# Feed-forward parts with quarter products: the weight steps are handed out more densely, up to four at a time

## The chip, the cores and the metric

The kernel runs as one program on 1 core of a Trainium2 chip. The metric is the device time of one execution in microseconds; the time shown of a kernel is the median of three executions. All numbers are float32; the matrix products are made of three matmuls each (high parts by high parts, low by high, high by low).

## The reference

512 tokens of width 1024 (16 more meta tokens stand ahead of them in the first block) go through two blocks: one with two layers, each with a feed-forward part, a mixer of attention and a gated recurrence, and a second feed-forward part; then one with a state space branch, an attention with a top-k choice, and a feed-forward part. What the change touches are four of the five feed-forward parts:

```python
D_MODEL = 1024; SEQ = 512; DEPTH = 2; N_META = 16; D_FF = 2816

def swiglu(x, w_gu, w_down):
    gate, up = jnp.split(x @ w_gu, 2, axis=-1)
    return (jax.nn.silu(gate) * up) @ w_down

for l in range(DEPTH):
    h = h + 0.5 * swiglu(rms_norm(h, ffn1_norm[l]), ffn1_w_gu[l], ffn1_w_down[l])   # a0, a1
    ...                                                                             # the mixer
    h = h + 0.5 * swiglu(rms_norm(h, ffn2_norm[l]), ffn2_w_gu[l], ffn2_w_down[l])   # b0, b1
...                                                                                 # the second block
x = x + (jax.nn.silu(h2 @ w_ffn_gate[l]) * (h2 @ w_ffn_up[l])) @ w_ffn_down[l]      # c
```

## The kernel before

Activations lie transposed: eight tiles `h` of 128 features by 528 tokens (512 in b1 and c). The hidden width of a feed-forward part is 22 slices of 128, called j = 0 to 21. For one slice the gate weights (1024 by 128) and the up weights are a chunk of 512 KB each; the down weights of a third of the slices (8, 7 and 7) and 128 outputs are a chunk of 512 or 448 KB. Chunks land in `raw` tiles, of which there are four (`RAW`, L285); a chunk is asked for when the fourth before it has been used up (`drop`).

Part a0 and the slices 0 to 5 of the others use plain products. In b0, a1, b1 and c the slices 6 to 21 are done by seven products of quarter size (`product`, L608): the two weight blocks are cut in halves over their inputs, and gate and up of one slice come out of seven products of four 128 by 128 weight tiles each, 12 matmuls of 264 (or 256) columns. The seven use three PSUM banks: b1 takes the products 0, 2, 4 and 6, b2 the product 1, b3 the products 3 and 5, each adding onto what stands there. Between two of them the bank is read out ("evacuated"): after product 0 and 2 ScalarE copies b1 to `tu`, after 3 it copies b3 to `zu`, after 1 and 5 VectorE adds into `c1`, after 4 and 6 into `c2`. So the bank of product i must have been read when product i+2 begins. After product 5 a Silu of `c1` follows, after product 6 two multiplications by it and a split of the result into `gh` (ScalarE) and `gl` (VectorE).

The products need sums and differences of weight halves, and all weights need a split into a high part `whi` (ScalarE) and a low part `wlo = w - whi` (VectorE here). This work is cut in steps (`steps_of`, L374): eleven for one slice, in this order: hi0a+s1, hi0b+s3, lo0, a2, hi1a+s4 (drops the gate chunk), hi1b+lo1a, hi2a+lo1b, hi2b+lo2a, lo2b, hi3, lo3 (drops the up chunk); and two, hi and lo, for a down chunk. The names: s1, s3, s4 and a2 are sums of 512 columns on VectorE, hi and lo are the splits of the weight sums 0 to 3 in halves a and b of 512 columns (lo0 takes 1024 at once). The split weights stand in a ring of five pairs of tiles (`H`, L284): the steps of the entry i may begin when the entry i-5 has been used by its last matmul (`allowed`, L425).

In the four parts the order on each engine is pinned: what is written first runs first. The list of the work is fixed: slices 6 and 7, then the slices 8 to 14 woven with the eight down parts of the first third, then 15 to 21 woven with those of the second third; the first four and the last four products of each such run stand alone. A down part is taken apart into items of one 128 by 128 weight tile, three matmuls of 512 columns or six of 264. After the matmuls of each product or item, and ahead of its evacuation, `between` is called (L436): the item's cost (1.46 or 0.73) is added to a credit, and as long as the credit is at least 1 and the ring allows it, the next step is written and takes 1 from the credit. Silu and the split of the slice before are written behind the first of these steps. Outside the four parts no credit is added, and steps run as far ahead as the ring allows.

Of the kernel before, what the change touches and what calls it, by code (L numbers as in the profile page):

```python
# [281 lines left out]
class Kernel:  # L282
# [46 lines left out]
    def run(self):  # L329
# [10 lines left out]
        credit = 0.0  # L340
# [84 lines left out]
        def allowed():  # L425
            if n_step == len(queue):
                return False
            i = queue[n_step][0]
            return i < self.H or done[i - self.H]

        def step():
            nonlocal n_step
            queue[n_step][1]()
            n_step += 1

        def between(cost):  # L436
            nonlocal credit
            credit = min(credit + cost / 0.9, 3.0)
            late, self.late = self.late, []
            while credit >= 1.0 and allowed():  # L440
                step()
                credit -= 1.0
                while late:
                    late.pop(0)()
            for fn in late:
                fn()
# [8 lines left out]
        for it in self.prog:  # L455
            if not (it.seven and self.pin):
                for i in range(used):
                    done[i] = True
            self.pin = it.seven
            if not it.seven:  # L460
                between(0.0)
                if it.chunks:
                    while allowed():
                        step()
            used += len(it.chunks)
            while n_step < len(queue) and queue[n_step][0] < used:
                assert allowed()
                step()
            it.fn()
# [1612 lines left out]
```

## Time and profile before

| | |
|---|---|
| median of three executions | 3180.65 us (3179.32 to 3181.38) |
| the profiled execution's own time | 3182.89 us |
| its span, first to last instruction | 3181.1 us |
| mean granted TensorE clock | 0.992 |
| TensorE busy | 3117.0 us (98%) |
| VectorE busy | 2074.8 us (65%) |
| ScalarE busy | 1378.3 us (43%) |
| GpSimd busy | 853.5 us (27%) |
| moved by DMA | 289.61 MB |

The profile is of one execution. PE is the matmul stream of TensorE, DVE is VectorE, ACT is ScalarE. Nearly all instructions carry the line of one helper (L249), so groups are told apart by the names of their tiles: `bank<-T2h,whi` is a matmul into PSUM. In the products T2h stands for the products 2 and 6, T1h for 3 and 4, B21h for 1 and 5, b11h for 0; `bank<-gh,...` are the down parts. Idle time behind an arrow is what the instruction waited for, and whose end it was. The duration of a matmul covers its way through the array; matmuls follow one another at a closer distance than that.

### The profile page before, as it was taken

How to read it: one execution, taken by the hardware profiler on the slowest of the kernel's cores; microseconds unless marked ns; L12 is line 12 of the kernel's file. 1: busy time of each engine (PE TensorE's matmuls, PEld its weight loads, DVE VectorE, ACT ScalarE, POOL GpSimd, SP SyncE). 2: the span in 40 equal slices, each digit the busy share in tenths (PEclk: the TensorE clock that was granted, in tenths of full speed). 3: DMA queues.
4: the chain of work that ended last, by engine and by line, in shares of the span. 5: the costliest groups of instructions: out<-in, count | busy, mean ns of one | idle time of the engine just before them, and what ended most of it. 6: DMA issues, size and time to landing. Idle time of an engine off the chain costs nothing. (4 is left out here: it accounts for less than half of the span.)

```text
span 3181.1 us, 52632 instructions
## 1 busy us (share of the span) xinstructions
PE 3117.0 (98%) x21530; PEld 2870.7 (90%) x21530; DVE 2074.8 (65%) x3552; ACT 1378.3 (43%) x2355; POOL 853.5 (27%) x493
## 2 busy tenths in 40 slices
PE   9999999999999999999999999999999989999999
PEld 9999999899999999999998888888998767888888
DVE  8664466763676667766666674577667795577674
ACT  5322345544344444444444553444446425444442
POOL 3453235543220002100034453330003543230001
PEclk9999999999999999999999999999999989999999
DMA  6333321111222233223332112222235332222332
GB/s 203 120 99 108 94 94 57 45 58 61 93 80 89 91 101 111 69 94 97 94 109 74 41 51 69 86 93 86 94 106 164 115 96 67 73 93 73 99 103 91
DMA packets 106530, 289.61 MB, mean 91 GB/s; under 512 B 23088, under 2 KB 32304, under 8 KB 106288
## 3 DMA queue, kind: packets, MB, share of 16 engines
q1 hardware_dynamic: 106288, 286.24, 28.5%
q8 instruction: 169, 2.77, 0.4%
q14 instruction: 73, 0.60, 0.1%
HBM read 272.96 MB, written 13.24 MB: 90 GB/s over the span
## 5 line engine op out<-in xcount | busy, mean ns | idle before, releaser
L249 POOL TENSOR_TENSOR wlo<-raw,whi 128x1024 fp32r<-128x1024 f32 (+1 forms) x217 | 542.7, 2503 | 1962.5 <-ACT whi L249 1665.4
L249 ACT ACTIVATE whi<-raw 128x1024 fp32r<-128x1024 f32 (+2 forms) x632 | 537.9, 866 | 813.5 <-PE bank L249 421.5
L249 PE MATMUL bank<-xh,whi 128*128 128x264 f32 (+1 forms) x2504 | 812.7, 325 | 5.3 <-DVE t L249 5.3
L249 PE MATMUL bank<-xl,whi 128*128 128x264 f32 (+1 forms) x2504 | 811.1, 324 | 4.7 <-DVE xl L249 4.4
L249 PE MATMUL bank<-xh,wlo 128*128 128x264 f32 (+1 forms) x2504 | 804.8, 322 | 1.3 <-POOL wlo L249 1.3
L249 PEld LDWEIGHTS bank<-xh,whi 128*128 128x128 f32 x2504 | 475.0, 190 | 35.6 <-DVE t L249 5.7
L249 PEld LDWEIGHTS bank<-xl,whi 128*128 128x128 f32 x2504 | 475.4, 190 | 34.8 <-DVE xl L249 6.6
L249 PEld LDWEIGHTS bank<-xh,wlo 128*128 128x128 f32 x2504 | 474.9, 190 | 26.9 <-issue 1.7
L249 PE MATMUL bank<-gh,wlo 128*128 128x264 f32 (+1 forms) x1408 | 440.6, 313 | 12.1 <-DVE wlo L249 12.1
L249 DVE TENSOR_TENSOR wlo<-raw,whi 128x1024 fp32r<-128x1024 f32 (+2 forms) x351 | 367.8, 1050 | 123.7 <-ACT whi L249 121.3
L249 PE MATMUL bank<-gh,whi 128*128 128x264 f32 (+1 forms) x1408 | 439.8, 312 | 0.0
L249 PE MATMUL bank<-gl,whi 128*128 128x264 f32 (+1 forms) x1408 | 439.7, 312 | 0.0
L249 PEld LDWEIGHTS bank<-gh,wlo 128*128 128x128 f32 x1408 | 265.3, 188 | 30.2 <-DVE wlo L249 14.6
L249 PEld LDWEIGHTS bank<-gl,whi 128*128 128x128 f32 x1408 | 265.3, 188 | 8.3
L249 PEld LDWEIGHTS bank<-gh,whi 128*128 128x128 f32 x1408 | 265.2, 188 | 8.4 <-issue 0.4
L249 ACT ACTIVATE p<-p,nm 128x144 f32<-128x144 f32 (+8 forms) x104 | 57.0, 548 | 227.3 <-DVE nm L249 222.4
L249 PE MATMUL bank<-T2h,whi 128*128 128x264 f32 (+1 forms) x512 | 146.5, 286 | 3.8 <-DVE c L249 3.5
L249 DVE SCALAR_TENSOR_TENSOR h<-bank,h 128x264 f32<-128x264 f32 (+1 forms) x192 | 88.7, 492 | 92.6 <-PE bank L249 91.6
L249 PE MATMUL bank<-T2h,wlo 128*128 128x264 f32 (+1 forms) x512 | 145.8, 285 | 1.8 <-DVE wlo L249 1.8
L249 PE MATMUL bank<-B21h,whi 128*128 128x264 f32 (+1 forms) x512 | 145.5, 284 | 0.9 <-ACT zu L249 0.9
L249 PE MATMUL bank<-B21h,wlo 128*128 128x264 f32 (+1 forms) x512 | 145.1, 283 | 0.0
L249 PE MATMUL bank<-T1h,wlo 128*128 128x264 f32 (+1 forms) x512 | 144.9, 283 | 0.0
(373 smaller groups left out, 6637.9 us busy)
## 6 DMA issues: line engine op xcount, KB each, us to landing
raw<-in_w_dram SPq DMA_DIRECT2D x423, 512.0 KB, 3.5
raw<-in_w_dram SPq DMA_DIRECT2D x80, 448.0 KB, 3.3
h<-in_x_dram SPq DMA_DIRECT2D x8, 264.0 KB, 6.0
s_t<-zero SPq DMA_DIRECT2D x8, 256.0 KB, 3.6
s_wo<-cm SPq DMA_DIRECT2D x16, 128.0 KB, 3.2
s_win<-cm SPq DMA_DIRECT2D x8, 256.0 KB, 2.0
s<-s_win SPq DMA_DIRECT2D x8, 256.0 KB, 4.4
s<-s_wo SPq DMA_DIRECT2D x8, 256.0 KB, 2.9
```

Of the source, the lines that this page charges most:

```text
L249: i = f(*args, **kw)
```

## The change

The divisor of the cost goes from 0.9 to 0.65, and the ceiling of the credit from 3 to 4. A product earns 1.46/0.65 = 2.25 steps and not 1.62, an item of a down part 1.12 and not 0.81, and after a time in which the ring allowed nothing up to four steps are written in one place and not three. The instructions are the same ones; what changes is where the steps stand among the evacuations.

```diff
         def between(cost):
             nonlocal credit
-            credit = min(credit + cost / 0.9, 3.0)
+            credit = min(credit + cost / 0.65, 4.0)
             late, self.late = self.late, []
             while credit >= 1.0 and allowed():
                 step()
```

## Rows read from the trace of the kernel before

**Rows 1.** The page's first part: busy us, share of the span, instructions by engine.
```profile
PE 3117.0 (98%) x21530; PEld 2870.7 (90%) x21530; DVE 2074.8 (65%) x3552; ACT 1378.3 (43%) x2355; POOL 853.5 (27%) x493
```
**Rows 2.** Waits of TensorE over the whole span: total us, times, longest.
```profile
PE bank L249 <- DVE wlo L249: 13.8, 16, 1.8
...
PE bank L249 <- DVE c L249: 3.5, 4, 0.9
```
**Rows 3.** Windows over b0 and c: busy PE, PEld, DVE, ACT, POOL; clock; DMA; GB/s.
```profile
960.00:1235.00 275.00, 270.33 (x2187) 268.51 (x2187) 180.34 (x305) 117.40 (x211) 7.00 (x3) 0.99 0.31 96
...
2880.00:3145.00 265.00, 260.45 (x1769) 239.07 (x1768) 179.75 (x290) 115.57 (x210) 7.13 (x3) 1.00 0.32 100
```
**Rows 4.** Waits of TensorE in c, 2880 to 3145 us.
```profile
PE bank L249 <- DVE wlo L249: 3.1, 4, 1.4
...
PE bank L249 <- DVE c L249: 0.8, 1, 0.8
...
PE bank L249 <- ACT zu L249: 0.4, 1, 0.4
...
PE bank L249 <- ACT tu L249: 0.2, 1, 0.2
```
**Rows 5.** Timeline of TensorE in c: start, us, instruction, idle before and releaser.
```profile
2944.33 0.50 PE L249 MATMUL bank<-gh,wlo 128*128 128x512 f32 x1 [1.45 <-DVE wlo L249]
...
3024.43 0.28 PE L249 MATMUL bank<-B21h,wlo 128*128 128x256 f32 x1
3025.53 0.38 PE L249 MATMUL bank<-T2h,whi 128*128 128x256 f32 x1 [0.82 <-DVE c L249]
3025.75 0.28 PE L249 MATMUL bank<-T2l,whi 128*128 128x256 f32 x1
```
**Rows 6.** Groups of VectorE in c by form: busy us, mean ns.
```profile
L249 DVE TENSOR_TENSOR wlo<-s,whi 128x512 fp32r<-128x512 f32 x45 | 29.3, 683 | 5.8 <-ACT whi L249 5.8
L249 DVE TENSOR_TENSOR wlo<-raw,whi 128x1024 fp32r<-128x1024 f32 x23 | 28.1, 1220 | 7.7 <-ACT whi L249 7.7
...
L249 DVE TENSOR_TENSOR wlo<-raw,whi 128x896 fp32r<-128x896 f32 x10 | 10.8, 1084 | 1.5 <-ACT whi L249 1.4
```
**Rows 7.** Groups of ScalarE in c by form.
```profile
L249 ACT ACTIVATE whi<-raw 128x512 fp32r<-128x512 f32 x61 | 36.2, 624 | 33.5 <-PE bank L249 18.1 <-issue 10.2 <-DVE raw L249 4.8
...
L249 ACT ACTIVATE whi<-raw 128x896 fp32r<-128x896 f32 x13 | 12.2, 945 | 6.9 <-DMA raw<-in_w_dram 5.4 <-PE bank L249 1.5
```
**Rows 8.** Timeline of VectorE in c, ahead of product 6 of slice 14.
```profile
3020.91 0.69 DVE L249 TENSOR_TENSOR wlo<-raw,whi 128x512 fp32r<-128x512 f32 x1 [2.76 <-ACT whi L249]
3021.52 0.68 DVE L249 TENSOR_TENSOR s<-raw 128x512 f32<-128x512 f32 x1
...
3023.32 1.22 DVE L249 TENSOR_TENSOR wlo<-raw,whi 128x1024 fp32r<-128x1024 f32 x1
3024.46 0.68 DVE L249 TENSOR_TENSOR raw<-s,raw 128x512 f32<-128x512 f32 x1
3025.06 0.42 DVE L249 TENSOR_TENSOR c<-bank,zu 128x256 f32<-128x256 f32 x1
```
**Rows 9.** Timeline of ScalarE and VectorE at the first product of c.
```profile
2889.66 0.63 ACT L249 ACTIVATE gh<-t 128x512 fp32r<-128x512 f32 x1 [5.35 <-DVE t L249]
2890.20 0.61 ACT L249 ACTIVATE whi<-raw 128x512 fp32r<-128x512 f32 x1
2890.33 0.69 DVE L249 TENSOR_TENSOR gl<-t,gh 128x512 fp32r<-128x512 f32 x1 [0.70 <-ACT gh L249]
2890.72 0.36 ACT L249 ACTIVATE tu<-bank 128x256 f32<-128x256 f32 x1
```
**Rows 10.** Windows around the longest stall of b0; columns as in the windows above.
```profile
1021.00:1024.00 3.00, 1.21 (x10) 0.99 (x9) 2.21 (x3) 2.59 (x6) 0.00 (x0) 1.00 0.01 3
1024.00:1028.00 4.00, 4.00 (x23) 4.00 (x22) 3.32 (x7) 1.58 (x2) 0.00 (x0) 0.57 0.74 262
1028.00:1032.00 4.00, 4.00 (x35) 4.00 (x34) 2.17 (x3) 1.02 (x2) 0.00 (x0) 1.00 0.29 69
```

## The prediction

> **What bounds the kernel now.** I read the page's busy shares first. TensorE is busy 3117.0 of 3181.1 us [rows 1], so what is left to win is its idle time, and of that only what lies where the credit is used. The waits of TensorE come next: 13.8 us for `wlo` and 3.5 us for `c` are the groups that belong to the quarter products [rows 2]. In part c alone they are 3.1 + 0.8 + 0.4 + 0.2 = 4.5 us in seven stalls [rows 4]; four such parts make 18, so the two groups lie wholly in them. The windows say the same: 270.3 of 275 us busy in b0, 260.5 of 265 in c, with VectorE at 66 to 68% and ScalarE at 43 to 44% [rows 3]. So neither helper engine lacks throughput; what counts is how long an evacuation stands in a queue.
>
> A stall costs more than its idle time. Before product 6 of slice 14 the idle time is 0.82, while the starts lie 1.10 and then 0.22 apart, where 0.12 is the usual distance (3025.75 less one) [rows 5]: 1.10 + 0.22 - 0.24 = 1.08, that is 0.27 more than the idle. For c that makes 4.5 + 7 x 0.27 = 6.4 us, for the four parts about 25. That is the most that any order of the steps could give back.
>
> **The change: what it can't touch.** The number of steps is the same, and steps were not short before. In a run of woven work 49 products and 64 items earn 49 x 1.62 + 64 x 0.81 = 131 steps, and 7 x 11 + 8 x 2 = 93 are there. So most of the time the ring holds the next step back, and the credit sits at its ceiling. Counting both kernels through item by item, no step is ever written at the last moment, and a step that waits for the ring is written behind the same matmul in both. The two long `wlo` stalls of each part (1.45 us at 2944.33 [rows 5], and 1.79 in b0 [rows 10]) are of this kind: the third down part of a third takes the ring place of the second, its hi and lo begin only after the last matmul of the second, and one product lies between. They stay.
>
> **What it moves.** A step that is written earlier stands ahead of an evacuation that it stood behind. On ScalarE a hi of 512 columns takes 0.62 us [rows 7] and the next begins 0.54 after its start (2889.66 to 2890.20 [rows 9]); on VectorE a split or sum takes 0.68 [rows 6] and the next begins 0.60 to 0.61 later (3020.91 to 3021.52), a lo of 1024 columns holds the queue for 1.14 (3023.32 to 3024.46 [rows 8]). An evacuation has the time of one product when products stand alone: 12 x 0.12 = 1.43 us. With down items between there is twice that, so the woven stretch has cover (0.1 to 0.3 in a few places). The places without it are the 18 products of slices 6, 7 and the first of 8, and slice 14's end with slice 15's beginning.
>
> Product 6 of slice 14, all four parts. VectorE's queue ahead of `c2` is now lo3, s1, the update of h, s3, lo0, a2 [rows 8], and TensorE waits 0.82. With up to four steps behind the last item, s3 goes ahead of h, and the next products take lo0 with a2, then s4 with lo1a: two more ahead of `c2`, 2 x 0.60 and some 0.1 of waiting for the hi. The stall grows by 1.3 to 1.4.
>
> Product 2 of slice 15, all four. The same slide puts d1.0's lo (1.08 [rows 6]) behind its hi (0.95 [rows 7]) ahead of product 5's `c1`; Silu, the two multiplications, `gh`, and then a hi3 follow before product 0's `tu`. From the end of `c2` that is about 5.2 us, the products take 4.3: 0.9 to 1.0 new.
>
> The beginning. From a1 on a credit of nearly 1 is left from the part before (0.98; in the kernel before 0.49), so product 0 writes three steps: hi0a comes between the hi at 2890.20 and `tu` [rows 9], 0.54 later. Then product 2's `tu` falls behind hi1a, which needs a2. VectorE comes to that from 2890.33 by gl, lo3, s1, s3, lo0, c1, a2: 4 x 0.60 + 1.14 + 0.34 + 0.68 = 4.6, to 2894.9; hi1a and `tu` end at 2895.9. Product 4 could start at 2891.14 + 0.54 + 0.11 + 2 x 1.43 = 2894.65: 1.25 lost, where nothing was. Product 2 of slice 7 loses 2.0: the pair of multiplications of slice 6 stands behind lo3, c1, s1, s3 and lo0 (3.3 us and about 1.3 of waits for their hi), and `tu` behind the `gh` that follows. In b0, which begins with credit 0, it is 0.9 and 0.75 before products 5 and 6 of slice 6 and 0.3 there. Product 2 of slice 8 loses 0.4 more in c, 0.7 in b0 (its `tu` behind a `gh` that comes late).
>
> The sum. I laid out the three queues of each part in issue order with these durations, both ways. New less old, in us: b0 0.9 + 0.75 + 0.3 + 0.1 + 0.7 + 1.4 + 0.9 - 0.1 = 4.9; a1 0.5 + 1.3 + 0.1 + 2.0 - 0.1 + 0.45 + 1.4 + 0.9 - 0.15 = 6.4; b1 and c each 0.5 + 1.4 + 0.1 + 2.1 - 0.5 (a wait for `zu` that goes) + 0.4 + 1.4 + 1.0 + 0.6 in the woven stretch = 7.0. Together 25.3. Laid out so, the kernel before loses 31 us, where the rows give some 25, so the sum may be a fifth too large: 20 to 25. I take 24, nearer the upper end, because the stalls that I could set against their rows one by one came within 0.2.
>
> What rides along costs nothing that I can find. Chunks are dropped earlier, so SP asks for the next ones earlier; the share of the DMA engines is 0.31 to 0.32 in these windows [rows 3]. If chunks came a microsecond late, ACT would wait with the evacuations behind it: some 3 us over all. The tail of a part writes three more down splits ahead of the last Silu; the first pair of plain down parts covers it with 12 weight tiles of three matmuls of 512 columns, at twice the 0.12 of 256 columns 8.6 us, and if that were gone, 1.6 us each part. It could also help: the splits for the plain part stand ready sooner; bound 0.2 each, which a wait before the last product shows in the tally. GpSimd has 3 instructions in a window [rows 3].
>
> **The clock.** After the stall of 1.79 us in b0 the granted clock was 0.57 over 4 us, between its two levels of 1.2 and 2.4 GHz, with 23 matmuls where the same time later takes 35: about 1.4 us lost. It had been 1.00 during the stall [rows 10]; none of the other long stalls was followed by this, c's window shows 1.00 [rows 3]. One in eight, of ten new stalls over 1.2 us, is one more drop, 1.4 us, and I leave it in the range. The Trainium skill, TensorE: Matmul & The Clock Gate, section "A second HAM failure mode: psum-queue depth-cycling", has it that frequent short idles between groups of matmuls, as banks are cycled, make the clock swing. By that rule each new stall would bring its own drop, 10 x 1.4 = 14 us on top; the trace so far speaks against it, seven times to one.
>
> From the profiled execution's 3182.9 (span 3181.1) the sum is 3206.9; it lies 2.2 above the median of the runs, so against 3180.65 it is 3204.7: I say 3205.
>
> **The rivals.** Stalls vanish: if the two long `wlo` stalls and the short one beside each came from steps that are written too late, denser steps end them. Gain in c 3.1 [rows 4] + 4 x 0.27 = 4.2, and some 17 in the four parts: 3164. It decides if the third down part's hi can start before the second's last matmul, that is, if a ring place is free. For it: they are waits for VectorE's `wlo` [rows 4]. Against it: the ring is as deep as before.
>
> Nothing happens: the ring sets the pace everywhere and the displaced evacuations keep cover, as in the woven stretch: 3181. For it: VectorE is idle a third of the time [rows 3]. Against it: `tu` at 2890.72 and `c2` at 3025.06 have no cover already now [rows 5, 9].
>
> Only slice 14's end counts: the beginnings catch up, since early lo's leave VectorE free later. 4 x (1.4 + 0.9) = 9: 3190.
>
> The clock follows each new stall: 3205 + 14 = 3219.
>
> **How the numbers follow.** Forecast 0.70, only slice 14 0.11, nothing 0.07, stalls vanish 0.05, the clock 0.07. The forecast's own spread is 20 to 25 and one or two drops, and below that beginnings that are half as bad (7 of the 15 in the sum): 3194 to 3209. The range leaves out the gains and no change and reaches into the other two: 3188 to 3216. 0.2% (6 us) is what a measurement of this kernel can tell from no change. Faster by more: the vanishing stalls, 0.05. Within: nothing, and a part of slice 14 alone, 0.09. Slower: 0.86.
>
> **What would show it.** Right: in each part the wait for `c` before product 6 of slice 14 goes from 0.8 to about 2.1, waits for ACT `tu` of 1 to 2 us appear before T2h and T1h (product 2 and 4) in the first 25 us of a1, b1 and c, and one of 0.6 or more before product 2 of slice 15; the long waits of `gh,wlo` stay at 1.2 to 1.8. In c the waits for `tu` grow from 0.2 [rows 4] to more than 3. Wrong: the `gh,wlo` waits shrink, the first 25 us of a part are as long as before, or the difference stands in windows outside the four parts.

## The result and the profile after

The changed kernel takes 3205.38 us, the median of four executions (3202.36 to 3210.03), against 3181.02 for the kernel before. The ratio is 1.0082, with a 95% interval of 1.007 to 1.0094: slower by 24 us. The prediction said 3205. The profiled execution took 3204.82 us, with a span of 3203.0.

Where the time went is seen first in the waits of TensorE over the whole span: total us, times, longest.

```profile
PE bank L249 <- DVE wlo L249: 13.8, 16, 1.8
PE bank L249 <- ACT tu L249: 13.0, 15, 1.7
...
PE bank L249 <- DVE c L249: 9.5, 5, 2.3
```

The same view of the kernel before has for `tu`:

```profile
PE bank L249 <- ACT tu L249: 0.4, 2, 0.2
```

The waits for `wlo` are the same to a tenth [rows 2]. Those for `c` have gone from 3.5 to 9.5 us, those for `tu` from 0.4 to 13.0. So TensorE does not wait longer for weights than before: what comes late is the reading out of a bank.

How long a part takes can be read from the first and the last start of one kind of matmul, here the products 2 and 6. The rows are those of T2h in b0, a1, b1 and c, count, min/median/max ns, first and last start. Before:

```profile
L249 PE MATMUL bank<-T2h,whi x128: 279/284/391, 969.5 to 1226.4; 128*128 128x264 f32 x128
L249 PE MATMUL bank<-T2h,whi x128: 280/283/388, 1342.1 to 1597.8; 128*128 128x264 f32 x128
L249 PE MATMUL bank<-T2h,whi x128: 276/279/387, 2169.3 to 2416.1; 128*128 128x256 f32 x128
L249 PE MATMUL bank<-T2h,whi x128: 277/281/388, 2891.1 to 3137.7; 128*128 128x256 f32 x128
```

After:

```profile
L249 PE MATMUL bank<-T2h,whi x128: 279/284/392, 968.9 to 1229.2; 128*128 128x264 f32 x128
L249 PE MATMUL bank<-T2h,whi x128: 280/283/390, 1344.8 to 1608.8; 128*128 128x264 f32 x128
L249 PE MATMUL bank<-T2h,whi x128: 277/281/387, 2181.3 to 2435.2; 128*128 128x256 f32 x128
L249 PE MATMUL bank<-T2h,whi x128: 276/281/581, 2906.4 to 3159.5; 128*128 128x256 f32 x128
```

The four parts took 256.9 + 255.7 + 246.8 + 246.6 = 1006.0 us and take 260.3 + 264.0 + 253.9 + 253.1 = 1031.3, which is 25.3 more. The wait ahead of the first of these matmuls lies outside of this measure; in a1, b1 and c it has grown by some 0.5 us each. The two spans differ by 21.9; the 3.4 us that the rest is shorter are within what single executions of either kernel differ by (7.7 us after).

Within c, the timeline of TensorE has new or longer stalls where the prediction had put them: ahead of product 2 of slice 6, product 4 of slice 6, product 2 of slices 7 and 8, and product 6 of slice 14. The fifth line, the first long `gh,wlo`, is the old stall, which stayed:

```profile
2906.43 0.39 PE L249 MATMUL bank<-T2h,whi 128*128 128x256 f32 x1 [0.72 <-ACT tu L249]
...
2910.70 0.39 PE L249 MATMUL bank<-T1h,whi 128*128 128x256 f32 x1 [1.15 <-ACT tu L249]
...
2919.84 0.39 PE L249 MATMUL bank<-T2h,whi 128*128 128x256 f32 x1 [1.72 <-ACT tu L249]
...
2930.71 0.39 PE L249 MATMUL bank<-T2h,whi 128*128 128x256 f32 x1 [0.46 <-ACT tu L249]
...
2963.16 0.49 PE L249 MATMUL bank<-gh,wlo 128*128 128x512 f32 x1 [1.47 <-DVE wlo L249]
...
3045.85 0.58 PE L249 MATMUL bank<-T2h,whi 128*128 128x256 f32 x1 [2.24 <-DVE c L249]
```

VectorE's timeline ahead of that last stall answers to [rows 8]:

```profile
3039.84 0.69 DVE L249 TENSOR_TENSOR wlo<-raw,whi 128x512 fp32r<-128x512 f32 x1 [2.42 <-ACT whi L249]
3040.45 0.68 DVE L249 TENSOR_TENSOR s<-raw 128x512 f32<-128x512 f32 x1
3041.05 0.69 DVE L249 TENSOR_TENSOR s<-raw,raw 128x512 f32<-128x512 f32 x1
3041.65 0.68 DVE L249 SCALAR_TENSOR_TENSOR h<-bank,h 128x512 f32<-128x512 f32 x1
3042.25 1.22 DVE L249 TENSOR_TENSOR wlo<-raw,whi 128x1024 fp32r<-128x1024 f32 x1
3043.38 0.69 DVE L249 TENSOR_TENSOR raw<-s,raw 128x512 f32<-128x512 f32 x1
3044.10 0.69 DVE L249 TENSOR_TENSOR s<-raw,raw 128x512 f32<-128x512 f32 x1
3044.77 0.69 DVE L249 TENSOR_TENSOR wlo<-raw,whi 128x512 fp32r<-128x512 f32 x1
3045.38 0.42 DVE L249 TENSOR_TENSOR c<-bank,zu 128x256 f32<-128x256 f32 x1
```

From the first lo to `c` it was 3025.06 - 3020.91 = 4.15 us, and is 3045.38 - 3039.84 = 5.54. The two rows at 3044.10 (s4) and 3044.77 (lo1a) are what has come in between. The engine goes from one instruction to the next without an idle stretch that the profile shows; the reader of the bank stands in the queue.

And ScalarE at the first product, answering to [rows 9]: a second hi (x2) now stands ahead of the first `tu`, and hi1a, which waits for its sum, ahead of the second.

```profile
2904.43 0.63 ACT L249 ACTIVATE gh<-t 128x512 fp32r<-128x512 f32 x1 [4.94 <-DVE t L249]
2904.97 1.14 ACT L249 ACTIVATE whi<-raw 128x512 fp32r<-128x512 f32 x2
2906.01 0.36 ACT L249 ACTIVATE tu<-bank 128x256 f32<-128x256 f32 x1
...
2909.74 0.63 ACT L249 ACTIVATE whi<-raw 128x512 fp32r<-128x512 f32 x1 [2.85 <-PE bank L249]
2910.28 0.37 ACT L249 ACTIVATE tu<-bank 128x256 f32<-128x256 f32 x1
```

The releaser of the row at 2909.74 is a matmul by the profile, but the last matmul ahead of it ends at 2909.55, and the sum a2 that this hi reads (`raw<-s,raw`) begins on VectorE at 2908.98 and takes 0.68: 2909.66. By these times it was the sum that ended the wait.

### The profile page after: what moved, and what is told of

Read it like the earlier page. It is cut to its first block, busy times and chain, and to the rows that moved or that the text cites. A ratio compares the mean times of both kernels' runs of the same rounds, so it can differ in the third digit from the quotient of the medians.

```text
span 3203.0 us, 52666 instructions
## 1 busy us (share of the span) xinstructions
PE 3121.8 (97%) x21530; PEld 2873.0 (90%) x21530; DVE 2066.2 (65%) x3552; ACT 1378.3 (43%) x2355; POOL 853.2 (27%) x493
## 5 line engine op out<-in xcount | busy, mean ns | idle before, releaser
L249 PE MATMUL bank<-T1h,whi 128*128 128x264 f32 (+1 forms) x512 | 145.1, 283 | 3.4 <-ACT tu L249 3.4
L249 PE MATMUL bank<-T2l,whi 128*128 128x264 f32 (+1 forms) x512 | 145.3, 284 | 0.0
## 6 DMA issues: line engine op xcount, KB each, us to landing
h<-in_x_dram SPq DMA_DIRECT2D x8, 264.0 KB, 7.4
```

The lines of the kernel that those rows point to most:

```text
L249: i = f(*args, **kw)
```

## The experiments

The theory: a step that is written ahead of an evacuation delays it by its own time, and this costs where the evacuation has only the time of one product. Its rivals: bunches of four cost and density doesn't; weights or chunks come late; the ring sets the pace whatever is written; the clock falls after new stalls and makes the loss. Kernels are named by divisor and ceiling. The sums of the four parts, read as above, are in the fifth column; the last has the stretches in these parts, in the profiled execution, in which the granted clock fell. The kernel before has one.

| kernel | median us | ratio to before (95%) | expected us | four parts, less before | clock drops |
|---|---|---|---|---|---|
| changed: 0.65, 4 | 3205.4 | 1.0082 (1.0070 to 1.0094) | 3205 | +25.3 | 3 |
| 0.65, 3 | 3198.7 | 1.0059 (1.0046 to 1.0071) | 3202 | +16.7 | 0 |
| 0.9, 4 | 3180.4 | 1.0001 (0.9992 to 1.0010) | 3184 | +0.6 | 0 |
| 0.65, 4 in woven stretches only | 3181.9 | 1.0002 (0.9993 to 1.0011) | 3185 | +2.2 | 1 |
| 0.65, 4, evacuation first | 3182.3 | 1.0009 (1.0000 to 1.0018) | 3187 | +5.8 | 2 |
| 0.55, 5 | 3245.7 | 1.0196 (1.0183 to 1.0209) | 3246 | +66.7 | 7 |
| 0.9, 3, evacuation first | 3173.2 | 0.9972 (0.9962 to 0.9982) | 3173 | -8.0 | 0 |
| 0.9, 3, Silu and split later | 3168.2 | 0.9959 (0.9947 to 0.9971) | 3170 | -12.4 | 0 |
| 0.9, 3, both orders | 3161.3 | 0.9934 (0.9921 to 0.9946) | 3162 | -17.9 | 0 |

What a drop costs can be read in the kernel before: b0 and a1 have the same stalls there (4.7 us of idle time each), b0 has the drop and takes 256.9 us, a1 has none and takes 255.7. That is 1.2 us, where the prediction worked out 1.4 from the matmuls [rows 10]. The changed kernel has two drops more than before, which is 2.4 to 2.8 of its 25.3 us: the clock as the main cost is ruled out. It also means that a part of the differences in the fifth column belongs to the clock wherever the last column is not 1.

**One half of the change each: the divisor alone, the ceiling alone.**

```diff
-            credit = min(credit + cost / 0.65, 4.0)
+            credit = min(credit + cost / 0.65, 3.0)
```

> Divisor 0.65 as in the changed kernel, ceiling 3 as before. Theory (an evacuation stands behind the steps written ahead of it; the ceiling acts only where a held-back bunch of steps is let go, at the end of slice 14): the wait for c before product 6 of slice 14 falls from 2.2-2.3 to about 1.6 us, all other new waits stay; 21 us over before, 3202, that is 3 to 4 under the changed kernel. Rival (bunches of four are what costs, the density alone is harmless): within 5 us of before, 3186 at most. Rival (clock drops after new stalls make most of the loss): not told apart by this run.

```diff
-            credit = min(credit + cost / 0.9, 3.0)
+            credit = min(credit + cost / 0.9, 4.0)
```

> Divisor 0.9 as before, ceiling 4 as in the changed kernel. Theory: only the wait for c before product 6 of slice 14 grows, from 0.8-0.9 to about 1.6 us, once in each of the four parts; 3 us over before, 3184; the beginnings of the parts keep their waits of before. Rival (bunches of four are what costs): 15 to 25 us over before.

With the divisor alone 3198.7, with the ceiling alone no difference that can be told from none. Waits of TensorE, divisor alone:

```profile
PE bank L249 <- ACT tu L249: 13.0, 17, 1.7
...
PE bank L249 <- DVE c L249: 6.8, 5, 1.6
```

Ceiling alone:

```profile
PE bank L249 <- DVE c L249: 6.3, 4, 1.6
...
PE bank L249 <- ACT tu L249: 0.4, 2, 0.2
```

The waits for `tu` belong to the divisor. The wait before product 6 of slice 14 is 0.8 to 0.9 with neither, 1.5 to 1.6 with one of the two and 2.2 to 2.3 with both, so the two edits add up there. Bunches of four as the main cost are ruled out. The divisor alone came out 3 us under what was expected; the paragraph on the clock below says where that may lie. For the ceiling alone, four stalls longer by 0.7 make 2.9 us, which the medians don't show; its interval ends 3 us above before, and its profiled execution lacks the drop of the clock that the one before has. These two kernels and the next two all came out 3 to 5 us under what was expected; why is open.

**Where the density costs.**

```diff
-        def between(cost):
+        def between(cost, alone=False):
             nonlocal credit
-            credit = min(credit + cost / 0.65, 4.0)
+            credit = min(credit + cost / (0.9 if alone else 0.65), 3.0 if alone else 4.0)
...
-            self.between(1.46)
+            self.between(1.46, j in (6, 7) or j in (8, 15) and i < 4 or j in (14, 21) and i >= 3)
```

> Divisor 0.65 and ceiling 4 for down items and for products woven with them; 0.9 and 3 for products that stand alone (slices 6 and 7, the first four of 8 and 15, the last four of 14 and 21). Theory (a step costs only where an evacuation has the time of a single product): 4 us over before, 3185; nothing new in the first 25 us of a part, the wait for c before product 6 of slice 14 at 1.6 to 1.7 since the bunch of four is let go just ahead of it. Rival (denser steps make weights late: they wait for the ring or for chunks with the evacuations behind them, wherever they are): most steps are written in the woven stretches, so most of the loss stays, 15 us or more over before.

Of the 24 us nothing is left that can be measured, though most steps are still written at the new density:

```profile
PE bank L249 <- DVE wlo L249: 13.8, 16, 1.8
PE bank L249 <- DVE c L249: 6.4, 4, 1.6
...
PE bank L249 <- ACT tu L249: 0.7, 2, 0.5
```

The four waits for `c` are those of the ceiling. Weights or chunks that come late are ruled out as the main cause: most of the loss would have stayed. ScalarE does wait longer for chunks in the changed kernel (43.0 us in all, 34.8 before), but these waits are 39.1 in the next kernel, whose loss is gone.

**The same density, the evacuation ahead of the steps.**

```diff
             seventh(ps, w, 4 * k0, ("B11", "B21", "T2", "T1", "T3", "B22", "T4")[i], start)
             if k0 or i == 6:
                 self.read(name)
-            self.between(1.46)
+            if i == 6:
+                self.between(1.46)
             if i == 0:
                 copy(tu[:, q0], ps, AF.Copy)
...
+            if i < 6:
+                self.between(1.46)
```

> Divisor 0.65 and ceiling 4, but for products 0 to 5 the evacuation is written ahead of the steps that the product earns (product 6 as it was, since it needs the Silu that is written with them). Theory (place in the queue): the waits for tu before products 2 and 4 go wholly, waits for c and zu of 0.2 to 1.3 remain in places where a step written one product earlier still stands ahead; 6 us over before, 3187, so three quarters of the loss is gone at the same density. Rival (steps that come too early wait for the ring or for chunks): the engines are held up by the waiting step whichever way, 20 us or more over before. Rival (clock): if new stalls go, drops go with them; same time as the theory, told apart only by the granted clock in the changed kernel's trace.

```profile
PE bank L249 <- DVE c L249: 3.6, 5, 0.9
PE bank L249 <- ACT zu L249: 2.2, 3, 0.9
...
PE bank L249 <- ACT tu L249: 1.0, 1, 1.0
```

With divisor and ceiling as in the changed kernel and the same instructions, the time is back at 3182.3. The place in the queue is the cause; this run shows it most directly. The edit moves more than the six evacuations, though: the Silu of a slice is now written with the steps of product 5 and not of product 6, and where products stand alone `gh` and `gl` come behind the next product's `tu`. So the run shows that the order is what costs, not what each of these places is worth. Two things were expected wrongly: a wait for `tu` of 1.0 us stays, before product 4 of slice 7 in b0, and the time is 5 us lower than said. The four parts in the table are those of one execution that took 3187.2.

**More of the same.**

```diff
-            credit = min(credit + cost / 0.65, 4.0)
+            credit = min(credit + cost / 0.55, 5.0)
```

> The suspected cost carried further in the same direction: divisor 0.55, ceiling 5. Theory (steps ahead of an evacuation, laid out as for the prediction): 65 us over before, 3246; the waits for tu, c and zu before products of slices 6, 7 and 14 grow to 1.8, 2.7 and 3.2 us, and now the woven stretch has new ones of 1 to 1.9 (products 2 or 6 of slices 11, 13, 18, 20). Rival (the ring sets the pace: once steps wait for it, writing them still sooner changes nothing): about the time of the changed kernel, 3205 to 3212.

```profile
PE bank L249 <- ACT tu L249: 24.5, 28, 2.3
...
PE bank L249 <- ACT zu L249: 11.6, 4, 3.0
PE bank L249 <- DVE c L249: 10.8, 12, 1.3
```

64 us over before, and the waits where they were laid out, those of the woven stretch too (1.27 us for `c` before product 6 of slice 11 in b1, at 2293.61). They are shorter than laid out: 1.6 to 1.7, 2.3 and 2.9 to 3.0 in slices 6, 7 and 14 where 1.8, 2.7 and 3.2 were said, and at most 1.3 in the woven stretch where 1 to 1.9 was said. Six drops of the clock more than before, some 7 to 8 us at the price above, were not in the layout. So that 3246 was met to the microsecond is partly luck. The cover of the woven stretch ends here: it holds for 0.65 and 4, not for any number. That the ring sets the pace and so nothing more can happen is ruled out.

**What the same reasoning gives back at the old density.** First the evacuations alone (the edit above, on the kernel before):

> Divisor 0.9 and ceiling 3 as before, evacuations of products 0 to 5 written ahead of the steps. Theory: the wait for c before product 6 of slice 14 and the 0.2 to 0.5 us at the beginnings go, the waits of the down parts for wlo stay (two of 1.2 to 1.8 and two of 0.2 in each part); 8 us less than before, 3173. Rival (what a place in the queue costs is only paid at a high density): same as before, 3181.

```profile
PE bank L249 <- DVE wlo L249: 13.8, 16, 1.8
```

No wait for `tu`, `zu` or `c` is left, and 8 to 9 us are gone, of which 1.2 to 1.4 can be the drop of the clock that the profiled execution before has. Then the order behind a held-back step:

```diff
             late, self.late = self.late, []
+            given = 0
             while credit >= 1.0 and allowed():
                 step()
                 credit -= 1.0
-                while late:
+                given += 1
+                while late and given >= 2:
                     late.pop(0)()
```

> Divisor 0.9 and ceiling 3 as before; Silu and the split of a slice into gh and gl are written behind the second of the steps of a place and not behind the first, so that a down part's lo no longer stands behind them. Theory (the two long waits of a part are hi, gh, gl and lo one after the other, after the ring place comes free): the waits of gh,wlo fall by 1.2 us each to 0.1 to 0.7; 11 us less than before, 3170. Rival (these waits are of the ring place alone, as the prediction put it): unchanged, 3181.

```profile
PE bank L249 <- DVE wlo L249: 4.5, 14, 0.6
PE bank L249 <- DVE c L249: 3.5, 4, 0.9
...
PE bank L249 <- ACT tu L249: 0.4, 2, 0.2
```

VectorE in c, at the first long `gh,wlo`, in this kernel:

```profile
2934.13 1.23 DVE L249 TENSOR_TENSOR wlo<-raw,whi 128x1024 fp32r<-128x1024 f32 x1 [1.19 <-ACT whi L249]
2935.27 0.68 DVE L249 TENSOR_TENSOR gl<-c,gh 128x512 fp32r<-128x512 f32 x1
```

and in the kernel before:

```profile
2942.44 0.69 DVE L249 TENSOR_TENSOR gl<-c,gh 128x512 fp32r<-128x512 f32 x1 [1.70 <-ACT gh L249]
2943.05 1.22 DVE L249 TENSOR_TENSOR wlo<-raw,whi 128x1024 fp32r<-128x1024 f32 x1
```

The lo now goes ahead of `gl`, directly behind its hi, and the stall falls from 1.45 to 0.33. So these waits were not of the ring place alone: 1.1 of the 1.45 us was a split that stood in the queue. Both together:

> Both edits of the order together, divisor 0.9, ceiling 3. Theory: the two add, 19 us less than before, 3162; in each part only two waits of gh,wlo of 0.3 to 0.7 and two of T2h,wlo of 0.2 are left. Rival (one edit takes away the cover of the other): no more than the better one alone, 3170 to 3173.

```profile
PE bank L249 <- DVE wlo L249: 4.5, 14, 0.6
```

They add: 3161.3 us, faster than both kernels, 0.66% under the one before. A deeper ring, which would show what is left of the two waits, was not tried.

## Why the prediction was right, point by point

The upper bound: right in kind. What any order of the steps could give back was put at 25 us; the two orders at the old density gave 18 of it in the four parts (21 in the medians), and the waits of these parts are down from 18.6 to 4.5 us. (In the prediction, 1.08 less 0.82 is 0.26 and not 0.27, and the row at 3025.06 stands in [rows 8]; neither changes a sum.)

What the change can't touch: the long `wlo` waits stayed (13.8 us, 16 times). The reason given was half of it. The hi does wait for the ring place, but between hi and lo stood `gh` and `gl`, and that could be changed. So the rival that these stalls vanish was rightly priced low for this change, with a reason that would have hidden a gain of 12 us from whoever had only the prediction.

Product 6 of slice 14: 1.3 to 1.4 more was said, 0.82 to 2.24 in c and 0.90 to 2.27 in b0 were measured, by the two instructions named. The beginnings, in c: 0.54 more was said before product 2 of slice 6, and 0.18 has become 0.72; 1.25 said before product 4, 1.15 measured; 2.0 before product 2 of slice 7, 1.72 measured, and 1.97 with the slower first matmuls counted as the prediction counts them. In b0 they were set too high: 0.9, 0.75, 0.3 and 0.7 were said, 0.64, 0.47, nothing and 0.40 measured.

Product 2 of slice 15: 0.9 to 1.0 was said for all four parts. In b0 and a1 it was 0.46 and 0.47, less than the 0.6 that was named as a sign; in b1 and c there is none. For b1 and c the clock may be the reason. After the stall of 2.24 us in c the granted clock fell; length, busy times, clock, DMA share, GB/s by window:

```profile
3040.00:3044.00 4.00, 3.61 (x31) 3.40 (x29) 4.00 (x6) 1.23 (x3) 0.00 (x0) 1.00 0.44 131
3044.00:3048.00 4.00, 2.15 (x10) 2.15 (x11) 3.63 (x7) 2.92 (x5) 0.00 (x0) 0.70 0.39 131
3048.00:3052.00 4.00, 4.00 (x32) 4.00 (x32) 3.90 (x9) 2.42 (x6) 0.00 (x0) 0.87 0.42 131
3052.00:3056.00 4.00, 4.00 (x34) 3.86 (x33) 3.05 (x6) 2.50 (x5) 0.00 (x0) 1.00 0.33 115
```

The products that follow ran slower, so the other engines had the time that was short. The kernel with the divisor alone, whose clock did not fall there (its ceiling differs too), has the wait:

```profile
3044.96 0.39 PE L249 MATMUL bank<-T2h,whi 128*128 128x256 f32 x1 [0.30 <-ACT tu L249]
```

The clock: one more drop was put into the range. The profiled execution has three in the four parts, where the one before has one [rows 10]: after the existing `gh,wlo` stall in a1, and after the stall before product 6 of slice 14 in b1 and c. The rival that it follows each new stall is wrong: eight other new or longer stalls over 1 us were followed by none. That the kernel with the divisor alone, without a drop in its parts, takes 8.6 us less in them, where 3 to 4 was expected, leaves about 4 us that the drops may have made; three of them at 1.2 to 1.4 us are that much. Whether the three drops come in each execution is open: over the whole program the mean granted clock of its four executions is 0.991 to 0.993, that of the kernel before 0.991 to 0.994.

The sum: 24 said, 24 measured, and 25.3 in the four parts of the profiled executions. The mechanism was right, place by place; that the sum is met to the microsecond is luck. Two errors offset each other: queue waits in slice 15 (3.8 said, 0.9 of idle time measured, some 1.5 with the slower first matmuls) and in the woven stretch (1.2 said, none to be seen) were set some 3.5 us too high, and the clock, two drops more of 1.2 to 1.4 us, was left out of the sum. The bound of 20 to 25 was too narrow for what it was made of.

## What to carry to other kernels

Background work that is written between a producer and its evacuation is not free because the engine has idle time: wherever the evacuation has less slack than the piece put ahead of it, the matrix engine waits for the difference. So before the density of such work is changed, count at which places the slack is one unit, and read the queue there. Better than tuning the density is the order: evacuate first, then the background step, and let a step that everybody waits for go ahead of those that nobody waits for yet; here that was worth 20 us, with no instruction added or removed.

## What the runs showed of the hardware

An instruction of VectorE or ScalarE that has nothing to wait for begins about 0.08 us before the profile's end of the one ahead (3040.45 + 0.68 = 3041.13, next start 3041.05), so queues are to be summed by starts and not by durations. A drop of the clock may come after a stall of 1.8 us and stay away after one of 2.27: in the changed kernel 3 of the 15 stalls over 1.2 us in the four parts were followed by one.
